# Two output projections of a RetNet and gMLP step recast as Strassen products, with another order of the LayerNorm behind them

## The chip, the core and the metric

The kernel runs on one core of a Trainium2 chip. A core has TensorE (PE in the rows, with its weight loads as PEld), VectorE (DVE), ScalarE (ACT), GpSimd (POOL) and SyncE (SP), which here only issues DMAs. The engines run each their own program and wait for one another on semaphores. The metric is the time on the device in microseconds, as the median of some runs: 1761.06 us before the change (three runs, 1760.05 to 1762.07).

## What is computed

One inference step of two layers, in fp32, for 1024 prompt tokens and 8 decode rows, model width 1024. Layer 1 is retention (four heads, gated), layer 2 a gated MLP of width 2048 with a spatial mix over chunks of 128 tokens. Both end in the same way:

```python
y = (silu(g) * o) @ w_out          # layer 1: [1024, 2048] @ [2048, 1024], the same for 8 decode rows
y = (u * mixed * silu(g)) @ w_out  # layer 2: the same sizes
x = layer_norm(ALPHA * x + y, ln_gain[i], ln_bias[i])
```

These two products are the "output projections". fp32 accuracy comes from splitting each operand into a high part, rounded to the matmul's format, and a low part, the rest; a product is then three matmuls: high by high, high by low, low by high (`mm3`, line 65).

## The kernel before

The order of all instructions is written out by hand (`manual_schedule`); each engine runs its own in that order. SBUF working tiles of 4 KB per partition come from one pool of `NSLOT` = 31 slots (`S`, line 53); an instruction that writes a new tile waits until an older one's last reader is done. PSUM has eight banks of 128x512 (`PS`).

Stages: the input projections of layer 1 (to about 585 us) with the decode state beside them; the retention in chunks (to 750.7); output projection `outb` with LayerNorm (from 750.7); the v projection of layer 2, pieces of `tm_piece` (from 949.6); u and g with the spatial mix, `fm_piece` (from 1146); output projection `outc` with LayerNorm (from 1544.4 to the end).

An output projection (class `OutProj`, lines 627 to 773) runs over four quarters q of the 2048 inner features and two halves n of the 1024 outputs. A piece (q, n) is 512x512 weights. `group` (line 652) multiplies one block of 128 tokens by it: four k-tiles by three terms, 12 matmuls of 512 columns into one bank, which DVE then adds to the tile `pre[tb]`, the residual (lines 662 and 664). `dec_group` does the same for the decode rows, 8 matmuls. So there are 8 pieces of 96 + 8 matmuls. The operands are split while the piece before runs: y by `ysplit` (ACT cast, then a subtraction on DVE or POOL), the weights by `wsplit` (line 123, ACT cast and DVE subtraction). `stream_step` loads and splits the weights of later pieces; `wload` issues the DMAs.

The last quarter is written out (lines 734 to 773): the left half leads the right one by two blocks, and after each right block comes that block's LayerNorm: `bn_stats` of both halves, `bn_aggr`, a power on POOL, `(x - mean) * gain` on DVE (line 702), `* rstd` on ACT (line 704), `+ bias` on POOL (line 708), and a store. In `outb` the finished blocks are transposed on PE (`x1_transpose`, line 782) into the operand of the next stage, some of them between the first groups of its first piece (`hook_x1`). `r_y` and `s_y` are the last transposes and gating of the stage in front, which lie among the first groups of a projection.

DVE's `nb` (line 602, 128x2) belongs to the retention stage: a group-norm bias, behind which ACT and then PE wait.

## Time and profile before

| | us |
|---|---|
| median of three runs | 1761.06 |
| profiled execution, span on the core | 1758.3 |
| PE busy in it | 1726.1 |
| DVE, ACT, POOL busy | 782.3, 537.6, 438.1 |
| `outb`: first matmul to the start of the second `tm` piece | 750.72 to 976.88 |
| `outc`: first matmul to the end of the span | 1544.42 to 1758.3 |
| mean granted TensorE clock | 0.994 |

The profile is of one execution; its span is from the first to the last instruction on the core, and durations are taken from it. A matmul's listed duration overlaps the next one's: how fast they follow one another is read from the starts, or from the chain, which merges a run of them. In the chain a row is the start, the duration and the count of a merged run. DVE instructions overlap by up to 0.1 us in the same way.

### The profile page before, as it was taken

How to read it: one execution, taken by the hardware profiler on the slowest of the kernel's cores; microseconds unless marked ns; L12 is line 12 of the kernel's file. 1: busy time of each engine (PE TensorE's matmuls, PEld its weight loads, DVE VectorE, ACT ScalarE, POOL GpSimd, SP SyncE). 2: the span in 40 equal slices, each digit the busy share in tenths (PEclk: the TensorE clock that was granted, in tenths of full speed). 3: DMA queues.
4: the chain of work that ended last, by engine and by line, in shares of the span. 5: the costliest groups of instructions: out<-in, count | busy, mean ns of one | idle time of the engine just before them, and what ended most of it. 6: DMA issues, size and time to landing. Idle time of an engine off the chain costs nothing.

```text
span 1758.3 us, 22771 instructions
## 1 busy us (share of the span) xinstructions
PE 1726.1 (98%) x9408; PEld 1522.0 (87%) x9408; DVE 782.3 (44%) x1149; ACT 537.6 (31%) x775; POOL 438.1 (25%) x276
## 2 busy tenths in 40 slices
PE   9999999999999999999999999999999999999995
PEld 9898888979999787877778977899999999987774
DVE  7134453533321577753368322154343343333358
ACT  4121424244432454531114222133323333411112
POOL 4122231411101666620026000012222221210116
PEclk9999999999999999999999999999999999999998
DMA  7135565555533544341113322234112221442212
GB/s 265 72 125 192 178 210 193 195 191 205 192 144 121 168 156 156 132 156 49 48 61 122 108 96 77 80 127 160 64 62 95 92 104 73 162 138 92 88 49 97
DMA packets 97703, 223.91 MB, mean 127 GB/s; under 512 B 8296, under 2 KB 43000, under 8 KB 97600
## 3 DMA queue, kind: packets, MB, share of 16 engines
q1 hardware_dynamic: 97392, 222.26, 36.2%
q8 instruction: 74, 1.21, 0.3%
q10 hardware_dynamic: 208, 0.20, 0.0%
q14 instruction: 29, 0.24, 0.0%
HBM read 152.83 MB, written 69.40 MB: 126 GB/s over the span
## 4 chain that ended last, share of the span: by engine, by line
PE 91%; DVE 3%; POOL 2%; issue 2%; DMA 1%; ACT 1%; SPq 0%; DVEq 0%; POOLq 0%; ACTq 0%
PE fm L63 41%; PE tm L63 20%; PE op L63 19%; PE o L63 2%; PE tmd L63 2%; PE pd L63 2%; PE mx L63 1%; PE st L63 1%; PE dps L63 1%; PE yt L1053 1%; DVE pre L702 1%; DVE nb L602 1%; POOL vl L495 1%; DMA qk<-qk_s 1%; PE y L618 1%
## 5 line engine op out<-in xcount | busy, mean ns | idle before, releaser
L63 PE MATMUL fm<-xh,wh 128*128 128x344 f32 x768 | 247.3, 322 | 0.7 <-ACT xh L300 0.7
L63 PE MATMUL fm<-xl,wh 128*128 128x344 f32 x768 | 246.4, 321 | 0.6 <-DVE xl L301 0.5
L63 PE MATMUL fm<-x1h,wh 128*128 128x344 f32 x768 | 246.9, 321 | 0.0
L63 PE MATMUL fm<-xh,wl 128*128 128x344 f32 x768 | 246.2, 321 | 0.0
L63 PE MATMUL fm<-x1h,wl 128*128 128x344 f32 x768 | 245.1, 319 | 0.0
L63 PE MATMUL fm<-x1l,wh 128*128 128x344 f32 x768 | 245.0, 319 | 0.0
L134 DVE TENSOR_TENSOR wl<-wr,wh 128x1024 fp32r<-128x1024 f32 x123 | 171.1, 1394 | 126.8 <-ACT wh L130 108.7
L63 PE MATMUL op<-wh,yh 128*128 128x512 f32 x512 | 202.4, 395 | 0.0
L63 PE MATMUL op<-wl,yh 128*128 128x512 f32 x512 | 201.6, 394 | 0.0
L63 PE MATMUL op<-wh,yl 128*128 128x512 f32 x512 | 201.6, 394 | 0.0
L130 ACT CAST wh<-wr 128x1024 fp32r<-128x1024 f32 x127 | 131.6, 1044 | 211.2 <-PE pd L63 98.0
L63 PEld LDWEIGHTS fm<-xh,wh 128*128 128x128 f32 x768 | 145.2, 189 | 4.7 <-ACT xh L300 1.1
L63 PEld LDWEIGHTS fm<-xl,wh 128*128 128x128 f32 x768 | 145.1, 189 | 2.7 <-DVE xl L301 1.2
L63 PEld LDWEIGHTS fm<-xh,wl 128*128 128x128 f32 x768 | 145.1, 189 | 0.0
L63 PEld LDWEIGHTS fm<-x1h,wh 128*128 128x128 f32 x768 | 144.3, 188 | 0.5
L63 PEld LDWEIGHTS fm<-x1l,wh 128*128 128x128 f32 x768 | 144.3, 188 | 0.4
L63 PEld LDWEIGHTS fm<-x1h,wl 128*128 128x128 f32 x768 | 144.2, 188 | 0.0
L664 DVE TENSOR_TENSOR pre<-pre,op 128x512 f32<-128x512 f32 x96 | 65.6, 684 | 137.6 <-PE op L63 137.6
L63 PEld LDWEIGHTS op<-wh,yh 128*128 128x128 f32 x512 | 96.1, 188 | 23.7
L63 PEld LDWEIGHTS op<-wh,yl 128*128 128x128 f32 x512 | 96.1, 188 | 22.7
L63 PEld LDWEIGHTS op<-wl,yh 128*128 128x128 f32 x512 | 96.1, 188 | 22.2
L412 DVE SCALAR_TENSOR_TENSOR dw<-s,qd_dec,dw 128x512 f32<-128x512 f32 x32 | 39.9, 1246 | 169.6 <-ACT dw L411 169.6
(204 smaller groups left out, 3062.4 us busy)
## 6 DMA issues: line engine op xcount, KB each, us to landing
wr<-in_w SPq DMA_DIRECT2D x127, 512.0 KB
s<-in_state SPq DMA_DIRECT2D x32, 512.0 KB
out_rs<-s SPq DMA_DIRECT2D x32, 512.0 KB
qk_s<-ro SPq DMA_DIRECT2D x16, 512.0 KB
v_s<-v SPq DMA_DIRECT2D x16, 512.0 KB
vbc<-vd_s SPq DMA_DIRECT2D x16, 512.0 KB
g_s<-g SPq DMA_DIRECT2D x16, 512.0 KB
qk<-qk_s SPq DMA_DIRECT2D x16, 512.0 KB
```

What stands on the lines that cost most here:

```text
L63: pe.matmul(out, lhs, rhs, start=start, stop=stop)
L130: act.copy(t, src)
L134: eng.tensor_tensor(t, src, f(W[p][half][0]), ALU.subtract)
L412: dve.scalar_tensor_tensor(w[:, 0, :], s[:, 0, :], qd_dec[:, h, 0, b:b + 1], w[:, 1, :], ALU.mult, ALU.add)
L495: pool.tensor_tensor(ll, src, f(hh), ALU.subtract)
L602: dve.scalar_tensor_tensor(nb, r["mv"][:, :, 0], -1.0, rs[:, 0:2], ALU.mult, ALU.mult)
L618: pe.transpose(ps[:, e * CH + ib * 128:e * CH + (ib + 1) * 128], on[:, ib, (2 * ep + e) * 128:(2 * ep + e + 1) * 128], ident)
L664: dve.tensor_tensor(dst, dst, ps, ALU.add)
L702: dve.scalar_tensor_tensor(t[:, cs], t[:, cs], mv[:np_, 0:1], gain[:, cs], ALU.subtract, ALU.mult)
L1053: pe.transpose(ps[:, k * 128:(k + 1) * 128], q["m"][half][:, k, blk * 128:(blk + 1) * 128], ident)
```

## The change

Each projection is done as two halves s of the inner features. A half is a product of a 2x2 block matrix A (two halves of the tokens by two quarters of features, cells `A(j, k)`) by a 2x2 block matrix B (two quarters of features by two halves of outputs), and is computed by Winograd's form of Strassen's identity: seven block products, p1 to p7, where there were eight. Each is cut into two `subs` c of 256 inner features, 28 subs in all. A sub takes its operands from `prep`: part 0 forms sums and differences of cells in place (on DVE and POOL), part 1 casts both operands on ACT, part 2 subtracts for A's low part on POOL, part 3 for B's on DVE. `prep` runs two subs ahead; for subs 18 to 27 its parts are spread evenly over subs 16 to 23.

In `group` one sub does 4 blocks of 128 tokens by 2 k-tiles by 3 terms. The products are chained in PSUM: p2 has bank set b; p5, then p3, go on in c; p1, p6, p7 and p4 go on in a. After each product DVE adds the bank to the output blocks (`evac`), and the next product of the chain accumulates onto the same bank. The decode rows use p2, p5, p3 and p1 and are added up in SBUF by DVE.

The last four subs (p7 and p4 of the second half) are interleaved by token block in eight steps, with the LayerNorm of all blocks behind them: blocks 0 to 3 are complete in front of the tail, 4 to 7 become complete in it. LayerNorm is now `x * rstd - mean * rstd` on ACT (Identity with bias), then gain and bias as two tensor instructions on DVE and POOL. In `outb` the split of the next weights (piece 32) is on DVE in steps 0 to 3 instead of POOL, and x1's transposes are at other places. In the retention stage the loads and splits of pieces 24 and 25 are replaced by `fetch` and `prep` of the first subs. `outc` reads y back in cells, most of them into the two large buffers that held x1. The pool has 33 slots, and the descriptor scratch of software DMAs is set to 1024 bytes.

The core of the diff, of long stretches the new lines only:

```diff
+NSLOT = 33
...
+    PROJ = (*range(24, 32), *range(56, 64))
+    HOLD_LOAD, HOLD_SPLIT = (*PROJ, 32, 33), (*PROJ, 32)
...
     class OutProj:
+        ORDER = ("p2", "p5", "p3", "p1", "p6", "p7", "p4")
+        CHAIN = {"p2": "b", "p5": "c", "p3": "c", "p1": "a", "p6": "a", "p7": "a", "p4": "a"}
+        OUT = {"p2": (0, 0), "p5": (1, 1), "p3": (0, 1), "p1": (0, 0), "p6": (0, 1), "p7": (1, 1), "p4": (1, 0)}
+        ACELL = {"p2": (0, 1), "p5": (1, 0), "p3": (0, 1), "p1": (0, 0), "p6": (1, 0), "p7": (0, 0), "p4": (1, 1)}
+        BCELL = {"p2": (1, 0), "p5": (0, 1), "p3": (1, 1), "p1": (0, 0), "p6": (0, 1), "p7": (0, 0), "p4": (1, 0)}
...
+            self.subs = [(s, x, c) for s in range(2) for x in self.ORDER for c in range(2)]
...
+        def fetch(self, i):
...
+            s, x, c = self.subs[i]
+            for k in {"p2": ((1, 0),), "p5": ((0, 1), (0, 0)), "p3": ((1, 1),)}.get(x, ()):
+                t = self.b[s, k, c] = S(f"wr{self.p0}_{s}{c}_{k[0]}{k[1]}", (128, 2, 512))
+                sp.dma_start(t, a["w"][self.p0 + 2 * (2 * s + k[0]) + k[1], c])
+        def prep(self, i, part=None):
...
+            s, x, c = self.subs[i]
+            def A(j, k):
+                return self.cell(s, j, k, c)
+            def B(j, k):
+                return self.b[s, (j, k), c]
+            def sub(eng, out, in0, in1):
+                eng.tensor_tensor(out, in0, in1, ALU.subtract)
+            if part == 0:
+                if x == "p5":
+                    pool.tensor_tensor(A(1, 0), A(1, 0), A(1, 1), ALU.add)
+                    sub(dve, B(0, 1), B(0, 1), B(0, 0))
+                if x == "p3":
+                    sub(dve, A(1, 0), A(1, 0), A(0, 0))
+                    sub(pool, A(0, 1), A(0, 1), A(1, 0))
+                if x == "p6":
+                    sub(dve, B(0, 1), B(1, 1), B(0, 1))
+                if x == "p7":
+                    sub(pool, A(0, 0), A(1, 1), A(1, 0))
+                    sub(dve, B(0, 0), B(0, 1), B(0, 0))
+                if x == "p4":
+                    sub(dve, B(1, 0), B(1, 0), B(0, 1))
+                return
+            src = A(*self.ACELL[x]), B(*self.BCELL[x])
+            if part == 1:
+                hl = []
+                for n, t in zip("yw", src):
+                    hl.append([S(f"{n}{k}{self.p0}_{i}", (128, 2, 512), F32R) for k in "hl"])
+                    act.copy(hl[-1][0], t)
+                self.op[i] = hl
+            else:
+                hh, ll = self.op[i][part - 2]
+                sub(pool if part == 2 else dve, ll, src[part - 2], f(hh))
...
+        def group(self, i, pair):
+            s, x, c = self.subs[i]
+            ch = self.CHAIN[x]
+            first = c == 0 and x in ("p2", "p5", "p1")
+            if first:
+                self.ps[ch, pair] = PS(f"op{self.p0}_{s}{ch}_{pair}")
+            ps = self.ps[ch, pair]
+            (ah, al), (bh, bl) = self.op[i]
+            sl = slice(pair * 128, (pair + 1) * 128)
+            for k in range(2):
+                mm3(ps, ah[:, k, sl], al[:, k, sl], bh[:, k, :], bl[:, k, :], first and k == 0, c == 1 and k == 1,
+                    skip=x not in ("p2", "p5", "p1"))
+        def evac(self, i, pair):
+            x = self.subs[i][1]
+            j, n = self.OUT[x]
+            tb = 4 * j + pair
             dst = self.pre[tb][:, n * 512:(n + 1) * 512]
+            ps = self.ps[self.CHAIN[x], pair]
+            if (tb, n) not in self.seen:
+                self.seen.add((tb, n))
                 dve.scalar_tensor_tensor(dst, dst, ALPHA, ps, ALU.mult, ALU.add)
             else:
                 dve.tensor_tensor(dst, dst, ps, ALU.add)
...
         def dec_pre(self, n):
...
+            r8 = small.tile([NB, 512], F32, tag="r8", name=f"r8pd{self.p0}_{n}")
+            dve.tensor_tensor(r8, self.acc[n][:8, :], self.t8[n], ALU.add)
+            dve.scalar_tensor_tensor(dst, dst, ALPHA, r8, ALU.mult, ALU.add)
+            self.ln_half(TB, n)
...
+        def ln_stats(self, tbs):
...
+            for i, tb in enumerate(tbs):
+                dve.bn_aggr(mv[:np_, i, :], self.st.pop(tb)[:np_])
+            dve.tensor_scalar(r[:np_, 0, :n], mv[:np_, :n, 1], EPS, None, ALU.add)
+            pool.tensor_tensor(r[:np_, 1, :n], r[:np_, 0, :n], mhalf[:np_, :n], ALU.pow)
...
+            def nb():
+                dve.scalar_tensor_tensor(r[:np_, 2, :n], mv[:np_, :n, 0], -1.0, r[:np_, 1, :n], ALU.mult, ALU.mult)
...
+        def ln_z(self, tb, cuts=1):
+            rs, nb = self.L.pop(tb)
+            t = self.pre[tb]
+            for cs in self.cut(cuts):
+                act.activation(t[:, cs], t[:, cs], AF.Identity, bias=nb, scale=rs)
+        def ln_gain(self, tb, eng):
+            t = self.pre[tb]
+            eng.tensor_tensor(t, t, self.gain[:NB] if tb == TB else self.gain, ALU.mult)
+        def ln_bias(self, tb, eng, fin):
+            t = self.pre[tb]
+            eng.tensor_tensor(t, t, self.bias[:NB] if tb == TB else self.bias, ALU.add)
+            fin(tb, t, slice(0, D))
...
+        def run(self, fin, extra, last, early):
+            tail = len(self.subs) - 4
+            ahead = 16
+            queue = [(i, part) for i in range(ahead + 2, tail + 4) for part in range(4)]
+            done = 0
+            for i in range(tail):
+                s, x, c = self.subs[i]
+                for pair in range(4):
+                    run_later()
+                    if i < 2:
+                        self.pre_load(4 * i + pair)
+                    if i == 2 and pair == 0:
+                        self.pre_load(TB)
+                    if pair == 0:
+                        self.fetch(i + 4)
+                    if i < ahead:
+                        self.prep(i + 2, pair)
+                    else:
+                        to = len(queue) * (4 * (i - ahead) + pair + 1) // (4 * (tail - ahead))
+                        for j, part in queue[done:to]:
+                            self.prep(j, part)
+                        done = to
...
+                    if i == tail - 2:
+                        if pair >= 2:
+                            self.dec_pre(pair - 2)
+                    if i == tail - 1:
+                        if pair == 0:
+                            self.ln_stats([TB])
+                        if pair == 2:
+                            self.nb()
+                            self.ln_z(TB)
+                        if pair == 3:
+                            self.ln_gain(TB, dve)
+                            self.ln_bias(TB, pool, fin)
+                    early(i, pair)
+                    self.group(i, pair)
+                    if c == 1:
+                        self.evac(i, pair)
+                        if s == 1 and x == "p1":
+                            self.ln_half(pair, 0)
+                        if s == 1 and x == "p6":
+                            self.ln_half(pair, 1)
...
+                if s == 1 and x == "p1" and c == 1:
+                    self.dec_fold()
+            self.ln_stats(range(4))
+            for step, (k, pair) in enumerate(((0, 0), (0, 1), (2, 0), (0, 2), (2, 1), (0, 3), (2, 2), (2, 3))):
                 run_later()
+                tb = 4 + pair
+                for c in range(2):
+                    self.group(tail + k + c, pair)
+                self.evac(tail + k + 1, pair)
+                self.ln_half(tb, 0 if k else 1)
+                if step in (0, 3, 5, 7):
+                    self.nb()
+                if k:
+                    self.ln_stats([tb])
+                for z in {0: (0,), 1: (1,), 2: (2,), 3: (4, 3), 5: (5,), 7: (6,)}.get(step, ()):
+                    self.ln_z(z)
+                if step in (0, 1, 2, 3, 4, 5, 7):
+                    self.ln_gain((0, 1, 2, 4, 3, 5, None, 6)[step], dve if step else pool)
+                if step:
+                    self.ln_bias((None, 0, 1, 2, 4, 3, 5, 6)[step], pool, fin)
+                extra(step)
+            self.nb()
+            self.ln_z(7, 2)
+            t = self.pre[7]
+            for cs in self.cut(2):
+                dve.tensor_tensor(t[:, cs], t[:, cs], self.gain[:, cs], ALU.mult)
+                dve.tensor_tensor(t[:, cs], t[:, cs], self.bias[:, cs], ALU.add)
+                if last:
+                    fin(7, t, cs)
+            if not last:
+                fin(7, t, slice(0, D))
...
-    def extra_b(tb):
-        if tb >= 3:
-            x1_transpose()
-        if tb == 7:
-            x1_transpose()
-        if tb == 0:
+    def extra_b(step):
+        if step < 4:
+            wsplit(32, step, eng=dve)
+        if step in (3, 5):
+            x1_transpose(step // 2 - 1)
+        if step == 5:
             wload(33)
...
         r_load(n + 3)
-        if n == NS - 5:
-            wload(24)
-        if n == NS - 4:
-            wload(25)
-        if n >= NS - 4:
-            wsplit(24, n - NS + 4, eng=pool)
-        if n == NS - 1:
-            for t2 in range(4):
-                outb.ysplit(0, t2)
-            outb.pre_load(0)
-            outb.pre_load(1)
+        if NS - 6 <= n < NS - 2:
+            outb.fetch(n - NS + 6)
+        if n >= NS - 2:
+            outb.prep(n - NS + 2)
...
+    def r_last(i, pair):
+        if (i, pair) == (0, 3):
             r_y(NS - 1)
+        if (i, pair) == (21, 3):
+            wload(32)
...
+    x1_transpose(2)
+    x1_transpose(3)
...
     def hook_x1(i):
+        tb = {0: 4, 2: 5, 3: 6, 4: 7, 5: TB}.get(i)
+        if tb is not None:
+            x1_transpose(tb)
...
+    YC, YB = {}, {}
+    def cell_c(s, i, j, c):
+        if (s, i, j, c) not in YC:
+            if s not in YB:
+                YB[s] = xp.tile([128, KT, T], F32, tag="x", name=f"yb{s}")
+            YC[s, i, j, c] = YB[s][:, 4 * j + 2 * c:4 * j + 2 * c + 2, i * 512:(i + 1) * 512]
+        return YC[s, i, j, c]
+    def yload_c(s, i, j, c, own=False):
+        if own:
+            YC[s, i, j, c] = S(f"ly{i}{j}{c}", (128, 2, 512))
+        sp.dma_start(cell_c(s, i, j, c), y_s[2 * s + j][:, 2 * c:2 * c + 2, i * 512:(i + 1) * 512])
+    outc = OutProj(56, cell_c, y1d, x1_s.rearrange("t p d -> (t p) d"), x1d_s, 1)
...
+                if i in (0, 1):
+                    yload_c(0, 0, 1, i, own=True)
+                    outc.fetch(i)
+                if i in (2, 3):
+                    outc.fetch(i)
+                    outc.prep(i - 2)
                 if i == 4:
+                    yload_c(0, 1, 0, 0, own=True)
+                    yload_c(0, 1, 1, 0, own=True)
         fm_piece(40 + 2 * g, x1["h"], x1["l"], ug_evac(g, AF.Gelu, "u"), per_group=hook_u)
...
+    def early_c(i, pair):
+        if i == 0:
+            if pair == 0:
+                for j in (0, 1):
+                    yload_c(0, 1, j, 1)
+            if pair == 1:
+                yload_c(0, 0, 0, 0)
+                yload_c(0, 0, 0, 1)
+            if pair >= 2:
+                s_y(GR - 1, pair - 2)
+        if i == 2:
+            k, c = ((0, 1, 0), (1, 0, 0), (1, 1, 0), (0, 0, 0))[pair], 0
+            yload_c(1, k[0], k[1], 0)
+            yload_c(1, k[0], k[1], 1)
...
-    outc.run(fin_c, lambda tb: None, True, last_y)
+    outc.run(fin_c, lambda step: None, True, early_c)
-    nc = bacc.Bacc("TRN2", target_bir_lowering=False, num_devices=1)
+    nc = bacc.Bacc("TRN2", target_bir_lowering=False, num_devices=1, dynamic_dma_scratch_size=1024)
```

## Rows read from the trace of the kernel before

**Rows 1.** The page: busy time, share and instructions of each engine; the chain that ended last, by engine.

```profile
PE 1726.1 (98%) x9408; PEld 1522.0 (87%) x9408; DVE 782.3 (44%) x1149; ACT 537.6 (31%) x775; POOL 438.1 (25%) x276
...
PE 91%; DVE 3%; POOL 2%; issue 2%; DMA 1%; ACT 1%; SPq 0%; DVEq 0%; POOLq 0%; ACTq 0%
```

**Rows 2.** The chain that ended last, in order of time: start, duration, engine, tile, line and count of a merged run; `op` are the projection's matmuls, `pd` its decode matmuls, `tm` those of the next stage.

```profile
750.72 8.35 PE op L63 x36
...
773.87 1.84 PE pd L63 x8
775.71 22.27 PE op L63 x96
...
799.82 22.21 PE op L63 x96
...
976.88 22.78 PE tm L63 x192
...
1544.42 5.55 PE op L63 x24
```

**Rows 3.** The end of the span: the last matmul and the last DVE instructions of the timeline (start, duration, engine, line, operation, operands, count), and the sum of the windows from 1735 to 1758 (us, then busy time of each engine).

```profile
1738.73 0.39 PE L63 MATMUL op<-wh,yl 128*128 128x512 f32 x1
...
1750.54 2.93 DVE L708 TENSOR_TENSOR pre<-pre,lnb 128x512 f32<-128x512 f32 x2 [0.56 <-ACT pre L704]
...
sum 23.00, PE 4.11 PEld 3.00 DVE 17.11 ACT 4.67 POOL 12.09; mean PE 1.03 PEld 0.75 DVE 4.28 ACT 1.17 POOL 3.02
```

**Rows 4.** The timelines of POOL and DVE at 649 us (retention), at 757 us and in the LayerNorm of the second projection, in order of time within each place; in brackets the idle time in front and what ended it.

```profile
648.90 2.37 POOL L495 TENSOR_TENSOR qkl<-qk,qkh 128x1024 fp32r<-128x1024 f32 x1
648.96 2.32 DVE L602 SCALAR_TENSOR_TENSOR nb<-mv,rsrn 128x2 f32<-128x2 f32 x1 [0.21 <-POOL rsrn L254]
...
756.83 0.16 DVE L602 SCALAR_TENSOR_TENSOR nb<-mv,rsrn 128x2 f32<-128x2 f32 x1 [0.87 <-POOL rsrn L254]
...
1726.82 1.28 DVE L702 SCALAR_TENSOR_TENSOR pre<-pre,lmv,lng 128x1024 f32<-128x1024 f32 x1
...
1731.52 2.39 POOL L708 TENSOR_TENSOR pred<-pred,lnb 8x1024 f32<-8x1024 f32 x1
1732.35 5.53 DVE L702 SCALAR_TENSOR_TENSOR pre<-pre,lmv,lng 128x1024 f32<-128x1024 f32 x1
1733.88 0.54 POOL L254 TENSOR_TENSOR rsrl<-rstl,mhalf 128x1 f32<-128x1 f32 x1
1734.40 2.39 POOL L708 TENSOR_TENSOR pre<-pre,lnb 128x1024 f32<-128x1024 f32 x1
```

**Rows 5.** The timelines of POOL and DVE in the LayerNorm of the first projection: a drain that reads PSUM and SBUF, and statistics that read one tensor.

```profile
921.45 2.40 POOL L708 TENSOR_TENSOR pre<-pre,lnb 128x1024 f32<-128x1024 f32 x1 [1.26 <-ACT pre L704]
922.32 0.67 DVE L664 TENSOR_TENSOR pre<-pre,op 128x512 f32<-128x512 f32 x1
923.03 0.69 DVE L685 BATCH_NORM_STATS2 lst<-pre 128x6 f32<-128x512 f32 x1
```

**Rows 6.** Casts and subtractions of 128x1024: the group of ACT's weight casts (count, busy us, mean ns, idle before), and from the timelines DVE's subtraction beside POOL's and alone, and a POOL instruction that began beside one of DVE.

```profile
L130 ACT CAST wh<-wr 128x1024 fp32r<-128x1024 f32 x127 | 131.6, 1044 | 211.2 <-PE pd L63 98.0 <-PE op L63 57.4 <-DVE wl L134 14.9
...
750.71 2.97 DVE L641 TENSOR_TENSOR yl<-yT,yh 128x1024 fp32r<-128x1024 f32 x1 [0.38 <-ACT yh L640]
...
763.41 1.22 DVE L134 TENSOR_TENSOR wl<-wr,wh 128x1024 fp32r<-128x1024 f32 x1
...
1728.48 3.09 POOL L708 TENSOR_TENSOR pre<-pre,lnb 128x1024 f32<-128x1024 f32 x1
```

**Rows 7.** One decode step on DVE from the timeline, and two groups of ACT instructions (count, busy us, mean ns, idle before): LayerNorm's scaling, and `on`, an Identity with bias and scale.

```profile
912.98 0.68 DVE L679 SCALAR_TENSOR_TENSOR pred<-pred,r8pd 8x512 f32<-8x512 f32 x1
...
L704 ACT ACTIVATE pre<-pre,rsrl 128x1024 f32<-128x1024 f32 x15 | 17.3, 1152 | 78.7 <-POOL rsrl L254 50.8 <-DVE pre L702 27.9
...
L605 ACT ACTIVATE on<-o,nb,rsrn 128x512 f32<-128x512 f32 x32 | 23.2, 775 | 47.6 <-DVE nb L602 47.6
```

**Rows 8.** The chain again: a set of eight transposes of a block of x1, and those of its decode rows.

```profile
927.82 0.87 PE xt L800 x8
...
947.98 0.59 PE xtd L790 x8
```

**Rows 9.** TensorE after a gap in the retention stage: two rows of its timeline, and the window behind it (us, busy time and count of each engine, the granted clock, the DMA share and GB/s).

```profile
609.55 0.33 PE L618 MATMUL y<-ident,on 128*128 128x128 f32 x1 [2.33 <-ACT on L605]
...
611.43 0.63 PE L63 MATMUL o<-sl,qkh 128*128 128x512 f32 x1
...
610.00:615.00 5.00, 4.78 (x18) 3.93 (x19) 3.79 (x7) 1.53 (x3) 1.97 (x2) 0.66 0.43 158
```

**Rows 10.** The timelines of POOL and DVE at the end of the retention stage: a split of weight piece 24 and the `nb` beside it.

```profile
743.00 2.40 POOL L134 TENSOR_TENSOR wl<-wr,wh 128x1024 fp32r<-128x1024 f32 x1
743.07 2.35 DVE L602 SCALAR_TENSOR_TENSOR nb<-mv,rsrn 128x2 f32<-128x2 f32 x1 [0.81 <-POOL rsrn L254]
```

**Rows 11.** SP's DMA issues at the start of the first projection, and the window there (the last three columns are the clock, the DMA share and GB/s).

```profile
750.68 4.10 SPq L647 DMA_DIRECT2D pre<-in_x  x6
...
750.00:755.00 5.00, 5.00 (x24) 4.03 (x23) 4.62 (x6) 1.62 (x2) 5.00 (x2) 1.00 0.98 329
```

More of the change, by code (lines that the diff above doesn't have):

```diff
@@ L681, in ln_half @@
         def ln_half(self, tb, i):
             np_ = NB if tb == TB else 128
[L683 to L684 removed]
+            if tb not in self.st:
+                self.st[tb] = small.tile([128, 2, 6], F32, tag="lst", bufs=6, name=f"lst{self.p0}_{tb}")
             dve.bn_stats(self.st[tb][:np_, i, :], self.pre[tb][:, i * 512:(i + 1) * 512])
[L687 to L692 removed]
@@ L694, in ln_apply @@
-        def ln_apply(self, tb, fin, cuts=1):
-            np_ = NB if tb == TB else 128
-            t, gain, bias = self.pre[tb], self.gain[:np_], self.bias[:np_]
-            mv, rs = self.L[tb]
-            n = D // cuts
-            cut = [slice(i * n, (i + 1) * n) for i in range(cuts)]
-            for cs in cut:
-                dve.scalar_tensor_tensor(t[:, cs], t[:, cs], mv[:np_, 0:1], gain[:, cs], ALU.subtract, ALU.mult)
-            for cs in cut:
-                act.activation(t[:, cs], t[:, cs], AF.Copy, scale=rs[:np_, 0:1])
-            def add(eng):
-                for cs in cut:
-                    eng.tensor_tensor(t[:, cs], t[:, cs], bias[:, cs], ALU.add)
-                    fin(tb, t, cs)
-            return add
@@ new lines, in cut @@
+        def cut(self, n):
+            return [slice(i * (D // n), (i + 1) * (D // n)) for i in range(n)]
+        def ln_z(self, tb, cuts=1):
[10 more added lines that the diff above has]
+            fin(tb, t, slice(0, D))
```

202 lines of the change are left out of this document (60 added, 142 removed).

## Prediction

> **What bounds the kernel now.** I read the page's busy table first, then the chain that ended last, then the two projections in that chain, and last the queues of VectorE (DVE) and GpSimd (POOL) there. TensorE is busy 98% of the span and the chain is 91% PE [rows 1]; inside both projections it is one unbroken run of `op` matmuls, 22.21 to 22.27 us for 96 of them, so 0.232 us for one of 512 columns, with 1.84 us for the 8 decode matmuls behind each quarter [rows 2]. So a matmul taken away is worth its 0.232 us as long as nothing else is late. The exception is the end: the last matmul begins at 1738.73, the span ends at 1758.3, and what runs between them is LayerNorm on DVE, POOL and ACT, with DVE busy 17.11 of 23 us [rows 3]. The retention stage before the first projection is the other place with PE gaps.
>
> DVE and POOL get in each other's way. A DVE instruction that reads two tensors from SBUF doesn't run while a POOL tensor instruction runs: the 128x2 `nb` took 2.32 us beside a POOL subtraction of 2.37 that began 0.06 earlier, and the 128x1024 LayerNorm step at 1732.35 took 5.53 against 1.28 alone, ending only after three POOL instructions [rows 4]. One that reads PSUM and SBUF isn't held: 0.67 us at 922.32 with POOL busy from 921.45 to 923.85, and so are the statistics [rows 5]. I call the first kind two-input work.
>
> The Trainium skill ("SBUF — State Buffer", section "Who interferes with whom") has a rule for this, which speaks against the change: DVE with two SBUF inputs and GpSimd share a port under an exclusive lock, held for a whole instruction. The rows above agree (2.32 for an instruction of 0.16). Without this rule the sum would be the faster rival's below, with it the forecast's.
>
> **The change, part by part.** Durations are those of the profiled execution, span 1758.3; the median of the runs is 1761.06, so 2.8 us lie around the span, and I add them at the end.
>
> *Matmuls.* A projection has 8 quarters of 96 matmuls, 768; after, 28 sub-products of 4 row blocks, 2 k-tiles and 3 terms, 672. The decode matmuls stay at 64 (16 subs x 4). 96 x 0.232 = 22.3 us saved in each projection, 44.5 in both, if PE stays fed. A sub is 24 x 0.232 = 5.57 us, 6.50 with its decode part (0.93, half of 1.84). The first 16 subs take 10 x 6.50 + 6 x 5.57 = 98.4, the next 8 take 6 x 6.50 + 2 x 5.57 = 50.1, the tail's four 22.3. That an accumulation goes on in a bank just drained is shown by no row; from one group of the chain to the next nothing is lost (773.87 + 1.84 = 775.71 [rows 2]) and nothing can be gained, and a drain that comes late is counted below as a stall, so 0.
>
> *Operands.* Every sub splits an A and a B operand: two ACT casts (1.04 [rows 6]), one POOL subtraction, one DVE subtraction. Ten subs of a half also form sums: 10 on DVE and 6 on POOL. On POOL such a 128x1024 takes 2.37 [rows 4] to 3.09 where it waits for DVE; on DVE 1.22 alone, up to 2.97 beside POOL [rows 6]. I take 2.37 and 1.22 and count the waiting by the sum of both. In the first half this fits: a half has 20 POOL x 2.37 = 47 and 24 DVE x 1.22 = 29, 76 in its 85 us of PE. One place doesn't: behind p5 two products with two POOL steps each follow, and the A operand of p3 needs DVE, POOL, ACT, POOL in a row (1.22 + 2.37 + 1.04 + 2.37). DVE reaches p5's third drain some 4.9 us into p3, where PE wants the bank 2.8 us in: 2.1 us of stall, per projection.
>
> *The last eight subs (16 to 23)* prepare ten (18 to 27). POOL: 10 subtractions and 4 sums at 2.37, the decode bias 2.39 and a power 0.54 [rows 4]: 36.1. DVE two-input: 10 + 8 at 1.22, 4 decode steps at 0.68 [rows 7], a gain 1.28: 26. Sum 62 us where PE needs 50.1. The drains (16 x 0.69) and statistics (8 x 0.69) can lie beside POOL [rows 5], so DVE's own 46 isn't the bound; the pair is. DVE works in program order, so p6's last drains and statistics, for which LayerNorm waits, come at 62 after sub 16's start: 11.9 late. Bounds: 52 if POOL runs far ahead through the slots, 72 if each turn is lost (rivals).
>
> *LayerNorm tail.* From there, step by step in DVE's and POOL's orders: POOL a gain and seven biases at 2.37 and five powers at 0.54 [rows 4], 21.7; DVE six gains at 1.28 and four half-steps at 0.68, 10.4; the pair is full for 32, and idle 5.4 while the first drain, statistics, power and ACT's 1.15 run, and before the last ACT step. That is 37.4 to the last bias, and 4.8 to the end (the last DVE instruction of before ends at 1753.5, the span at 1758.3 [rows 3]). PE's last steps hide inside it. ACT's Identity with bias isn't there at 1024: 1.15 by Copy, 1.55 by twice 0.775 of `on` [rows 7]; I take 1.15, the row of its own size.
>
> *Second projection.* 98.4 + 1.7 (two sets of 8 transposes, 0.87 each [rows 8]) + 2.1 + 62 + 37.4 + 4.8 = 206.4. Before, 1544.42 to 1758.3 is 213.9 [rows 2, 3]. Minus 7.5.
>
> *First projection*, to the start of the second `tm` piece at 976.88: now 226.2 [rows 2]. After it there are transposes of x1, in PE's order; the one of block 3 stands in front of the `tm` groups, and waits for that block's bias, which POOL does fourth: 24.4 after DVE's 62 by the same walk, 26.8 with the two DVE splits of the next weights that now lie in the tail (2 x 1.22). Behind it: five sets of transposes at 0.87, the decode one 0.59 [rows 8], eight groups (22.78 [rows 2]) and 1.87 for decode, 29.6. PE has by then idled over 10 us, and after a gap of 2.3 us in the retention stage its granted clock was 0.66 over 5 us, with matmuls at the lower level (1.2 GHz), 0.63 instead of 0.39 [rows 9]: a third of 5 us, 1.7. 98.4 + 0.9 + 2.1 + 62 + 26.8 + 29.6 + 1.7 = 221.5. Minus 4.7.
>
> *Around it.* The four POOL splits of weight piece 24 leave the retention stage (one held `nb` for 2.35 at 743.07 [rows 10]), two POOL splits come: 0 to -2.3, I take -1. Loads: SP runs ahead of PE (six `pre` loads were issued in 4.1 us) at up to 329 GB/s [rows 11], 1.6 us for 512 KB. In the second projection the loads into `yb` wait for the last x1 matmul, and `pre` 1 to 3 stand behind two of them, four of them, and four and a store: at 1.6 each they land 5, 10 and 13 us in, and DVE wants them at 9.3, 10.7 and 12.1. DVE loses 1, which its slack there takes: 0, and 2 at most if the store is late. The smaller descriptor scratch: every transfer here is on the hardware queue, so 0; above, no PE wait on a DMA is in the trace, so a few tenths each on SP would still be hidden.
>
> Sum: -7.5 - 4.7 - 1 = -13.2; 1758.3 - 13.2 + 2.8 = 1747.9, so **1748**. Of 44.5 saved, some 31 is given back, nearly all to the DVE and POOL pair.
>
> **The rivals.**
> *Faster (PE stays the bound).* POOL's casts and sums mostly depend on nothing recent and could run ahead of DVE, so DVE finds the port free: DVE is done at 52, ten earlier in both. For: POOL is only 25% busy over the span. Against: 33 slots; nine `pre`, eight B cells and four operands for each sub in flight leave about four subs. 1748 - 2 x 10 = 1728; a tail that packs better reaches 1724.
> *Slower (DVE loses its turns).* Of the 24 two-input DVE instructions in the last eight subs some 0.6 find POOL busy (36 of 62) and wait 1.3 us each: 46 + 19, and 7 for ACT casts that come behind POOL, gives 72 instead of 62; PE, held by the drains, then loses the tail's rhythm too. Two projections: +20, 1768. It decides against the change from 68.6 on, where the 13.2 are gone. For: 5.53 for a step of 1.28 [rows 4]. Against: POOL too was made to wait: 3.09 instead of 2.39, where DVE had got in [rows 6].
> *No change*: DVE done at 67 to 70, half way, 1758 to 1764.
> *The change doesn't do what it says*: 512-column `op` matmuls not 3 x 448; nothing speaks for it.
>
> **How the numbers follow.** Forecast 0.42 (1738 to 1757), the faster rival 0.18, no change 0.16, the slower one 0.24. A difference of 0.2% (3.5 us) is about what can be told from none. Faster: 0.42 + 0.18 = 0.60; same 0.16; slower 0.24. The faster rival's floor of 1724 and the slower one's 1768 with 2 us for late loads and one more clock dip in each projection (2 x 1) bound the range: 1724 to 1772. The forecast's own is 1738 to 1757.
>
> **What would show it.** Right: `op` matmuls 3 x 448 of the same 0.39 us; PE unbroken to sub 16 but for stalls of about 2 us at p3; PE waiting for DVE's drains around the last eight subs; DVE subtractions of well over 1.22 mean and POOL at 2.4; from the last matmul to the end more than the 19.6 of before. Wrong: PE without waits until the tail (then it is the faster rival); stalls at p6 and p7 of the first half, or waits for slots in ACT's casts or for DMA at the start.

## The result, and the profile after

The changed kernel takes 1784.28 us (median of four runs, 1783.50 to 1785.79), the kernel before 1761.05 beside it: ratio 1.0131, 95% interval 1.0117 to 1.0146. The change costs 23 us; the forecast was 1748 and the range ended at 1772.

The profiled execution has a span of 1781.8. Its page, the lines that answer to [rows 1]; this chain reaches back over the last 96 us only:

```profile
PE 1700.1 (95%) x9216; PEld 1494.0 (84%) x9216; DVE 913.1 (51%) x1208; ACT 585.5 (33%) x820; POOL 605.1 (34%) x331
...
DVE 4%; ACT 0%; PE 0%; issue 0%; ACTq 0%; DVEq 0%
```

The 192 matmuls are gone as forecast, but PE has only 26 busy us less where 44.5 were expected, in part because it runs at its lower clock behind the longer gaps: the 384 matmuls of `op_1a` average 0.42 to 0.44 us where those of `op_0a` take 0.39. DVE has 131 us more, POOL 167. The end is no longer PE's: this chain is almost all DVE.

Where PE waits, from the list of waits (engine, tile and line, releaser; us in total, times, longest):

```profile
PE op_1a L63 <- DVE pre L731: 28.8, 8, 5.3
PE y L619 <- ACT on L606: 14.3, 15, 3.2
PE tm L63 <- DVE x1l L916: 6.8, 1, 6.8
PE op_0c L63 <- DVE pre L729: 4.8, 3, 2.6
PE op_1c L63 <- DVE pre L731: 4.3, 2, 2.2
```

`op_1a` are the products p1, p6, p7, p4 of the second half; line 731 is the drain that frees their bank. Every place but the second is new.

I divide both projections at rows that every version has: the first `op_0b` matmul, the first `op_1c` matmul (start of sub 16), DVE's fourfold `bn_aggr` (the statistics of blocks 0 to 3, behind p6's last drain), and for the first projection the first 512-column `tm` matmul, for the second the end of the span. PE's timeline of after in the second projection, its first and last rows and those with idle time in front:

```profile
1565.07 0.39 PE L63 MATMUL op_0b<-wh,yh 128*128 128x512 f32 x1
...
1593.77 0.47 PE L63 MATMUL op_0c<-wh,yh 128*128 128x512 f32 x1 [0.81 <-DVE pre L729]
...
1600.76 0.50 PE L63 MATMUL op_0c<-wh,yh 128*128 128x512 f32 x1 [2.57 <-DVE pre L729]
...
1670.62 0.40 PE L63 MATMUL op_1c<-wh,yh 128*128 128x512 f32 x1
...
1688.72 0.51 PE L63 MATMUL op_1c<-wh,yh 128*128 128x512 f32 x1 [2.15 <-DVE pre L731]
...
1718.29 0.50 PE L63 MATMUL op_1a<-wh,yh 128*128 128x512 f32 x1 [1.89 <-DVE pre L731]
...
1730.83 0.76 PE L63 MATMUL op_1a<-wh,yh 128*128 128x512 f32 x1 [5.33 <-DVE pre L731]
...
1742.29 0.77 PE L63 MATMUL op_1a<-wh,yh 128*128 128x512 f32 x1 [3.83 <-DVE pre L731]
...
1760.91 0.50 PE L63 MATMUL op_1a<-wh,yh 128*128 128x512 f32 x1 [1.64 <-DVE pre L731]
...
1763.57 0.40 PE L63 MATMUL op_1a<-wh,yl 128*128 128x512 f32 x1
```

Two windows of five us, one around the gap of 2.57 and one behind the gap of 3.83 (the granted clock is the third number from the end; behind the gaps the matmuls take 0.63 us for a while, the lower level, 1.2 GHz):

```profile
1599.80:1604.80 5.00, 4.04 (x11) 2.47 (x12) 3.65 (x3) 2.04 (x3) 4.71 (x2) 0.69 0.02 3
1743.00:1748.00 5.00, 5.00 (x14) 3.84 (x13) 3.82 (x4) 3.48 (x3) 3.63 (x2) 0.50 0.01 3
```

The forecast's terms in these stretches (its first projection ended at the second `tm` piece; that piece, 24.5 in both kernels, is added) and every version's, in us of one profiled execution; b and c are the first and the second projection:

| | subs 0 to 15, b / c | last eight, b / c | b: on to `tm` | c: on to the end | whole b / c | median |
|---|---|---|---|---|---|---|
| before | | | | | 250.6 / 213.9 | 1761.1 |
| forecast | 101.4 / 102.2 | 62 / 62 | 82.6 | 42.2 | 246.0 / 206.4 | 1748 |
| after | 107.4 / 105.6 | 69.7 / 69.7 | 94.0 | 41.4 | 271.2 / 216.7 | 1784.3 |
| e1 weights first | 105.7 / 100.7 | 68.6 / 68.6 | 94.0 | 41.4 | 268.3 / 210.7 | 1777.0 |
| e2 low by ACT | 101.8 / 100.3 | 60.9 / 59.4 | 95.1 | 41.4 | 257.8 / 201.1 | 1754.9 |
| e3 low on DVE | 103.8 / 103.9 | 66.4 / 66.4 | 94.6 | 41.8 | 264.8 / 212.1 | 1773.8 |
| e4 late transposes | 108.5 / 105.6 | 69.6 / 69.7 | 93.9 | 41.4 | 272.0 / 216.7 | 1786.0 |
| e5 x1 earlier | 107.5 / 105.6 | 69.7 / 69.7 | 87.0 | 41.5 | 264.2 / 216.7 | 1778.8 |
| e6 = e1 + e2 | 103.3 / 100.1 | 60.9 / 59.3 | 93.7 | 41.5 | 257.9 / 200.9 | 1755.2 |
| e7 late preps on DVE | 106.3 / 100.5 | 64.7 / 64.8 | 95.0 | 41.4 | 266.1 / 206.7 | 1769.8 |
| e8 four edits | 101.9 / 100.8 | 64.9 / 65.0 | 87.0 | 41.4 | 253.7 / 207.2 | 1757.6 |
| e9 decode in the tail | 107.5 / 106.8 | 63.4 / 63.5 | 102.7 | 48.8 | 273.7 / 219.1 | 1787.8 |
| e10 = e8 + e9 | 101.9 / 100.7 | 59.5 / 59.5 | 93.7 | 48.8 | 255.2 / 209.0 | 1761.3 |
| e11 = e10, earlier | 101.9 / 100.9 | 58.7 / 58.8 | 93.6 | 48.8 | 254.2 / 208.5 | 1759.7 |
| e12 = e8, nb on POOL | 101.9 / 100.6 | 64.9 / 65.2 | 86.0 | 37.4 | 252.8 / 203.3 | 1753.0 |

Where versions have the same code in a stretch, their cells differ mostly by under 0.5, and by 1.4 at most (b on to `tm`, e2 and e6).

What the forecast missed is 25.2 us in the first projection (6.0 + 7.7 + 11.4, rounded), 10.3 in the second (3.4 + 7.7 - 0.8), and the 1 us hoped for around them: 36.5 together, where 1784.3 is 36.3 from 1748. Only the LayerNorm tail of the second projection came out as summed.

### The profile page after: what moved, and what is told of

The parts are those of the page before. It is cut to its first block, busy times and chain, and to the rows that moved or that the text cites. A ratio compares the mean times of both kernels' runs of the same rounds, so it can differ in the third digit from the quotient of the medians.

```text
span 1781.8 us, 22544 instructions
## 1 busy us (share of the span) xinstructions
PE 1700.1 (95%) x9216; PEld 1494.0 (84%) x9216; DVE 913.1 (51%) x1208; ACT 585.5 (33%) x820; POOL 605.1 (34%) x331
## 5 line engine op out<-in xcount | busy, mean ns | idle before, releaser
L134 DVE TENSOR_TENSOR wl<-wr,wh 128x1024 fp32r<-128x1024 f32 x95 | 137.2, 1449 | 125.4 <-ACT wh L130 107.7
L671 DVE TENSOR_TENSOR wl<-wr,wh 128x1024 fp32r<-128x1024 f32 x56 | 113.3, 2028 | 61.9 <-ACT wh L693 61.9
L1133 POOL TENSOR_TENSOR vl<-lv,vh 128x1024 fp32r<-128x1024 f32 x16 | 40.9, 2553 | 261.7 <-ACT vh L1132 261.7
L421 POOL TENSOR_TENSOR dhl<-dw,dhl 128x512 fp32r<-128x512 f32 x32 | 43.2, 1351 | 242.1 <-ACT dhl L420 234.2
L63 PE MATMUL tm<-wh,x1h 128*128 128x512 f32 (+1 forms) x320 | 113.0, 353 | 6.9 <-DVE x1l L916 6.8
L63 PE MATMUL tm<-wl,x1h 128*128 128x512 f32 (+1 forms) x320 | 112.2, 351 | 0.0
L63 PE MATMUL tm<-wh,x1l 128*128 128x512 f32 (+1 forms) x320 | 112.1, 350 | 0.0
L130 ACT CAST wh<-wr 128x1024 fp32r<-128x1024 f32 x95 | 99.0, 1044 | 21.7 <-DMA wr<-in_w 15.7
L63 PE MATMUL tm<-wh,xh 128*128 128x512 f32 x256 | 101.0, 395 | 0.0
```

Of the source, the lines that this page charges most:

```text
L63: pe.matmul(out, lhs, rhs, start=start, stop=stop, skip_group_check=skip)
L130: act.copy(t, src)
L134: eng.tensor_tensor(t, src, f(W[p][half][0]), ALU.subtract)
L421: pool.tensor_tensor(hl[:, 1, :], w, f(hl[:, 0, :]), ALU.subtract)
L671: eng.tensor_tensor(out, in0, in1, ALU.subtract)
L1133: pool.tensor_tensor(ll, t, f(hh), ALU.subtract)
```

## Experiments

Four theories are weighed. P (port): POOL's instructions hold DVE's two-input ones. O (order): DVE idles for ACT's weight cast, which stands behind a y cast that waits for POOL. L (load): DVE has too much work of its own; L2: too much in subs 20 to 23. Q (queue): work that could go ahead stands behind LayerNorm in its engine's order. DVE's rows of after in the last eight subs of the second projection show signs of the first two:

```profile
1677.18 2.61 DVE L671 TENSOR_TENSOR wl<-wr,wh 128x1024 fp32r<-128x1024 f32 x1 [4.54 <-ACT wh L693]
...
1689.18 5.57 DVE L671 TENSOR_TENSOR wl<-wr,wh 128x1024 fp32r<-128x1024 f32 x2
...
1722.33 2.89 DVE L760 TENSOR_TENSOR r8pd<-acc,t8pd 8x512 f32<-8x512 f32 x1
...
1740.35 0.41 DVE L777 BATCH_NORM_AGGREGATE lmv<-lst 128x2 f32<-128x12 f32 x4
```

It idles 4.54 for a cast, and two subtractions of 1.22 take 5.57, a decode sum of 0.68 [rows 7] takes 2.89, beside POOL. (The expectations of e1 to e3 count the last eight subs to the end of the tail's first drain, 71.5 in after, 1.8 later than the table.)

**e1: weights cast first.**

```diff
-                for n, t in zip("yw", src):
...
-                    act.copy(hl[-1][0], t)
+                for n in ((1, 0) if x in ("p5", "p3", "p7") else (0, 1)):
+                    act.copy(hl[n][0], src[n])
```

> ACT casts the weight operand ahead of the y operand in the subs whose y operand is a sum formed on POOL (p5, p3, p7). Before this run the changed kernel shows DVE done with the last eight subs 71.5 us after sub 16's start: some 46 us of its own work, 16 in which its two-input instructions are stretched beside POOL, 9 idle for ACT's weight cast. Theory O (order: the weight cast stands on ACT behind a y cast that waits for POOL's sum): the idle stretches of 4.5 and 3.4 us go, and the stalls of PE at p3 shrink from 1.5 and 3.4 to under 1; both projections together 15 to 22 us less, 1762 to 1769. Theory P (port: POOL's instructions hold DVE): the idle time turns into waiting beside POOL, DVE is done at 67 to 71, and the time is 1775 to 1784. Theory L (DVE has too much work of its own in these subs): nothing changes, 1782 to 1786.

Measured 1777.0, ratio 1.0089 (1.0074 to 1.0104): P's case for the last eight (68.6), O's for p3, whose stalls are gone in both projections. DVE's groups (count | busy us, mean ns | idle before), of after:

```profile
L671 DVE TENSOR_TENSOR wl<-wr,wh 128x1024 fp32r<-128x1024 f32 x56 | 113.3, 2028 | 61.9 <-ACT wh L693 61.9
L671 DVE TENSOR_TENSOR wr<-wr,wr 128x1024 f32<-128x1024 f32 x32 | 68.0, 2126 | 0.0
L671 DVE TENSOR_TENSOR yb<-yb 128x1024 f32<-128x1024 f32 x3 | 3.6, 1209 | 0.0
```

and of e1:

```profile
L671 DVE TENSOR_TENSOR wl<-wr,wh 128x1024 fp32r<-128x1024 f32 x56 | 102.6, 1833 | 40.1 <-ACT wh L694 40.1
L671 DVE TENSOR_TENSOR wr<-wr,wr 128x1024 f32<-128x1024 f32 x32 | 72.7, 2273 | 0.0
L671 DVE TENSOR_TENSOR yb<-yb 128x1024 f32<-128x1024 f32 x3 | 9.1, 3019 | 0.0
```

Idle time for the cast falls by 22 us, and the three sums of `yb`, which ran alone before, now run beside POOL: 3.02 instead of 1.21 us.

**e2: y's low part by ACT** (28 subtractions of each projection are left out, a cast is in their place).

```diff
-                sub(pool if part == 2 else dve, ll, src[part - 2], f(hh))
+                if part == 2:
+                    act.copy(ll, src[0])
+                else:
+                    sub(dve, ll, src[1], f(hh))
```

> The low part of every y operand is written by an ACT cast in place of POOL's subtraction, so the subtraction is left out and POOL keeps the sums and LayerNorm. Theory P: DVE's weight subtractions fall from a mean of 2.03 us to 1.3 to 1.5, DVE is done with the last eight subs 52 to 58 us after sub 16's start instead of 71.5, and the time is 1745 to 1757. Theory O: the two idle stretches of 4.5 and 3.4 us stay, since POOL's sums still stand ahead of the y cast; DVE is done at 67 to 71 and the time is 1775 to 1784. Theory L: 1782 to 1786.

Measured 1754.9, ratio 0.9963 (0.9950 to 0.9976): 29 us less, as P has it. The same DVE instructions, with POOL busy 166 us less:

```profile
L671 DVE TENSOR_TENSOR wl<-wr,wh 128x1024 fp32r<-128x1024 f32 x56 | 70.9, 1267 | 69.0 <-ACT wh L693 67.5 <-PE op_1a L63 1.6
L671 DVE TENSOR_TENSOR wr<-wr,wr 128x1024 f32<-128x1024 f32 x32 | 43.8, 1369 | 0.0
```

The two groups lose 67 us of busy time, their idle time stays: the port is the larger loss. But the last eight take 60 (62 as the expectation counts), not 52 to 58.

**e3: y's low part on DVE**, nothing left out.

```diff
-                sub(pool if part == 2 else dve, ll, src[part - 2], f(hh))
+                sub(dve, ll, src[part - 2], f(hh))
```

> POOL's subtraction for the low part of every y operand moves to DVE, 28 of 1.22 us in each projection, ten of them in the last eight subs. Theory L: DVE has 46 + 12 of its own in these subs and loses what it lost before, done at 80 to 84, the time 1800 to 1810. Theory P: POOL holds DVE for 2.4 with each subtraction that DVE does in 1.22 itself; without them DVE has 58 of its own, some 3 to 5 beside POOL's sums, and is done at 61 to 66, the time 1765 to 1775. Theory O: the two idle stretches stay but are partly filled with the moved work: 1784 to 1795.

Measured 1773.8, ratio 1.0072 (1.0057 to 1.0087): P's case by its time; the last eight, 66.4 (68 as the expectation counts), lie a little above its 61 to 66. DVE gets 56 instructions more, its busy time stays (913.0 against 913.1 on the page), and the kernel takes 10.5 us less. That rules out L as the whole cause: DVE does each in 1.32 to 1.69 on the mean, where POOL needs 2.4 and more.

**e6: e1 and e2 together.**

```diff
+                for n in ((1, 0) if x in ("p5", "p3", "p7") else (0, 1)):
+                    act.copy(hl[n][0], src[n])
...
+                if part == 2:
+                    act.copy(ll, src[0])
```

> Both earlier edits: weights cast first, and the y operand's low part by an ACT cast, so POOL's subtraction is left out. One alone brought the last eight subs from 69.7 to 68.6 (order), the other to 60.9 and 59.4 us (port). If the idle time for ACT's cast is a second loss that only shows once POOL no longer holds DVE, both together bring the last eight to 51 to 55 and the time to 1739 to 1746. If the idle time is no loss of its own (DVE has 46 of its own and the sums' chain on POOL sets the rest), the last eight stay at 58 to 61 and the time is 1749 to 1755.

Measured 1755.2, ratio 0.9970 (0.9958 to 0.9982), not apart from e2: order isn't a second loss in the last eight. What is left there shows in the windows of subs 16 to 19 and 20 to 23 (us, then busy time and count of PE, PEld, DVE, ACT, POOL; granted clock, DMA share, GB/s):

```profile
1652.30:1678.50 26.20, 26.20 (x115) 19.75 (x114) 15.87 (x19) 14.53 (x15) 12.29 (x4) 1.00 0.00 1
1678.50:1711.60 33.10, 29.89 (x128) 22.83 (x126) 28.93 (x40) 15.01 (x15) 1.64 (x2) 1.00 0.10 33
```

and, for the same subs, in those of after:

```profile
1670.62:1699.04 28.42, 26.27 (x114) 19.48 (x113) 20.52 (x16) 9.67 (x10) 19.70 (x7) 1.00 0.00 1
1699.04:1740.35 41.31, 32.19 (x129) 24.23 (x127) 39.67 (x42) 11.63 (x12) 22.81 (x9) 0.92 0.08 26
```

In e6 DVE is busy 15.9 us in the first four subs, where PE needs 26.2, and 28.9 in the next four, with POOL out of them (1.64), where PE needs 2 x 6.50 + 2 x 5.57 = 24.1. Of after's 41.3 there, DVE is busy 39.7: those 28.9 and 10.7 more, beside a POOL that is busy 22.81. And POOL is idle for the other 18.5: the two engines together are not full there, DVE is. The slack of the first four is of no use to the next.

**e7: e1, and the late preparation on DVE.**

```diff
+                late = dve if i >= 18 else pool
...
+                n = part - 2 if i < 18 or x not in ("p5", "p3", "p7") else 3 - part
+                hh, ll = self.op[i][n]
+                sub(pool if n == 0 and i < 18 else dve, ll, src[n], f(hh))
```

> Weights cast first, and for subs 18 to 27 the y operand's sums and low parts on DVE, so that POOL takes no part in the preparation of the last eight subs; the computation is whole. Theory P: DVE has 46 + 14 x 1.22 = 63 of its own there and nothing holds it: last eight 62 to 65 instead of 69.7, first sixteen as with weights first alone, time 1764 to 1769. Theory L (DVE's load alone sets it): the last eight grow to 80 and more, 1795 to 1805. If a chain of sums and casts sets it, 66 as with the low parts alone on DVE, 1771 to 1775.

Measured 1769.8, ratio 1.0051 (1.0036 to 1.0066): last eight 64.7 and 64.8, P's case; the time is 1 us above it. In subs 20 to 23 of the second projection DVE is as full as in after, with POOL almost out of it:

```profile
1687.41:1726.37 38.96, 32.25 (x129) 24.33 (x127) 38.19 (x49) 10.28 (x10) 1.71 (x2) 0.91 0.08 28
```

**e9: the decode rows' LayerNorm in the tail** (on after; their statistics, scaling, gain and bias move to steps 3 to 6 with it).

```diff
-                    if i == tail - 2:
-                        if pair >= 2:
-                            self.dec_pre(pair - 2)
...
+                if step in (1, 3):
+                    self.dec_pre(step // 2)
```

> The changed kernel with one edit: the decode rows' last sums and their LayerNorm (some 6 us of DVE's own work, 8.5 with the 2.9 us that one of them took beside POOL) leave subs 22 and 23 for the tail, where DVE idles 1.1 to 1.3 us at a time for ACT. With weights first and the low parts on ACT, DVE was busy 15.9 of 26.2 us in subs 16 to 19 and 28.9 of 33.1 in subs 20 to 23, where PE's own work is 24. Theory L2 (DVE's own work is uneven: too much in subs 20 to 23): the last eight fall from 69.7 to 61 to 64, the tail grows by 1 to 3, both projections together 9 to 14 less, 1770 to 1775. Theory P alone (the pair's sum sets it, wherever the work stands): the last eight fall by 6 and the tail grows by 5 or 6, so 1782 to 1785.

Measured 1787.8, ratio 1.0149 (1.0132 to 1.0166). The last eight fall by 6.3, to 63.4 and 63.5, but both theories say that. They part at the tails, which grow by 8.7 and 7.4: more than was moved, near P's 5 or 6 and far from L2's 1 to 3, and the time lies above both. So this run doesn't decide for L2; that DVE's own work is uneven stands on the windows of e6. The idle bits that I counted on are no room: PE now waits 7.73 us for one drain in the second tail (before 1763.37), where after's longest wait there is 3.83.

**e4: the retention stage's last transposes three groups later.**

```diff
-        if (i, pair) == (0, 3):
+        if (i, pair) == (1, 2):
             r_y(NS - 1)
```

> The last transposes of the retention stage stand three groups later in PE's order (36 op matmuls ahead of them as in the kernel before, instead of 18). If the 3.23 us that PE waits there, and the matmuls at the lower clock behind it, are the change's own loss: 3 to 5 us less, 1779 to 1781. If the wait only moves, since the first preps of DVE, POOL and ACT hold the rows that the transposes read: 1783 to 1786.

Measured 1786.0, ratio 1.0139 (1.0122 to 1.0155): no gain. PE's wait at `y` is gone, and these are new in p5 and p3 (PE's timeline of e4):

```profile
769.46 0.50 PE L63 MATMUL op_0c<-wh,yh 128*128 128x512 f32 x1 [1.28 <-DVE pre L729]
...
784.62 0.47 PE L63 MATMUL op_0c<-wh,yh 128*128 128x512 f32 x1 [3.33 <-DVE pre L729]
...
791.61 0.50 PE L63 MATMUL op_0c<-wh,yh 128*128 128x512 f32 x1 [1.03 <-DVE pre L729]
```

DVE was late at p3 anyway. Where it isn't, the same edit does pay: from e7 to e8, which differ in it and in e5's edit (that one acts later), subs 0 to 15 fall from 106.3 to 101.9.

**e5: x1's blocks 2 and 3 ahead of the last block's LayerNorm.** Rows of after there, of POOL (the biases of blocks 4 and 3), of PE (its last wait in the tail, the transposes of blocks 2 and 3, its wait in `tm`) and of ACT; PE's wait of 6.77 follows from ACT's late casts:

```profile
953.43 4.73 POOL L802 TENSOR_TENSOR pre<-pre,lnb 128x1024 f32<-128x1024 f32 x2
...
953.69 0.79 PE L63 MATMUL op_1a<-wh,yh 128*128 128x512 f32 x1 [5.03 <-DVE pre L731]
...
957.87 1.91 PE L911 MATMUL xt<-ident,pre 128*128 128x128 f32 x16
...
973.44 0.58 PE L63 MATMUL tm<-wh,x1h 128*128 128x256 f32 x1 [6.77 <-DVE x1l L916]
...
965.26 1.24 ACT L794 ACTIVATE pre<-pre,lrs 128x1024 f32<-128x1024 f32 x1 [7.20 <-DVE lrs L782]
967.86 1.52 ACT L794 ACTIVATE pre<-pre,lrs 128x512 f32<-128x512 f32 x2 [1.36 <-DVE lrs L782]
969.29 2.02 ACT L915 CAST x1h<-xt 128x512 fp32r<-128x512 f32 x4
```

```diff
-        if step in (3, 5):
-            x1_transpose(step // 2 - 1)
+        if step in (3, 5, 6, 7):
+            x1_transpose((3, 5, 6, 7).index(step))
...
-    x1_transpose(2)
-    x1_transpose(3)
```

> In the first projection the transposes of x1's blocks 2 and 3, with their ACT casts and DVE subtractions, stand in the tail's steps 6 and 7, ahead of the last block's LayerNorm, instead of behind it. Theory Q (the queue): PE waited 6.77 us at the first tm group because these casts and subtractions stood on ACT and DVE behind the last block's LayerNorm, which they don't need. Then that wait falls under 1, the stretch from the four-block statistics to the 512-column tm piece falls from 94.0 to 87 to 89 us, and the time to 1777 to 1780; the second projection doesn't change. Rival (LayerNorm itself is late): the wait comes back at the transposes of a later block, and the time is 1782 to 1785.

Measured 1778.8, ratio 1.0102 (1.0085 to 1.0118): Q's case. The casts come 12 us earlier, counted from DVE's fourfold `bn_aggr` (927.98 in after, 930.09 in e5), and PE's wait is 0.59 (rows of ACT and of PE):

```profile
959.14 2.03 ACT L915 CAST x1h<-xt 128x512 fp32r<-128x512 f32 x4
...
962.03 0.39 PE L63 MATMUL tm<-wh,x1h 128*128 128x256 f32 x1 [0.59 <-DVE x1l L916]
```

**e8: four edits, the whole computation.**

```diff
+                for n in ((1, 0) if x in ("p5", "p3", "p7") else (0, 1)):
...
+                late = dve if i >= 18 else pool
...
+        if step in (3, 5, 6, 7):
...
+        if (i, pair) == (1, 2):
```

> The whole computation with four edits: weights cast first, late preparation on DVE, x1's blocks 2 and 3 ahead of the last block's LayerNorm, and the retention stage's last transposes three groups later. If the gains add up: 1784 - 7 (weights first) - 10 (late preparation) - 6 (x1) - 3 (transposes, now that DVE isn't late at p3) = 1758, 1755 to 1761, a little under the kernel before. If the stalls only move between the four places: 1764 to 1772.

Measured 1757.6, ratio 0.9982 (0.9972 to 0.9991): the gains add up.

**e10 and e11: a fifth edit, and preparation spread from sub 10 on.**

```diff
+                if step in (1, 3):
+                    self.dec_pre(step // 2)
...
-            ahead = 16
+            ahead = 10
```

> The four edits that gave 1757.6, and the decode rows' LayerNorm in the tail as a fifth. By theory L2 the last eight fall from 64.9 to 57 to 60, the tail grows by 1 to 2: 1745 to 1750. If the tail's DVE work is what ends last, the gain is given back there: 1753 to 1758.

> The five edits, and the ten preparations of the last subs begin to spread at sub 10 instead of 16, so that subs 10 to 23 prepare 16 subs and the last eight a little over nine instead of ten. If DVE's own work in subs 20 to 23 is still the bound there, a half to one preparation less (1.5 to 3 us) in each projection: 1741 to 1747. If the 33 slots are too few for operands that are made earlier, waits for slots appear on ACT or SP: 1750 or more.

Measured 1761.3, ratio 1.0000 (0.9991 to 1.0009), and 1759.7, ratio 0.9992 (0.9982 to 1.0001). As in e9 the last eight gain what was moved, 5.4, and the tails give back more, 6.8 and 7.4; 1761.3 is above both of e10's ranges. The earlier spread takes 0.8 off the last eight, less than expected; its 1.6 us in the median are within what can't be told from none. The time lies where waits for slots were expected, but e10, without the earlier spread, isn't faster.

**e12: e8, and LayerNorm's shift on POOL.** In e8 the handover in the tail looks like this (DVE, then ACT):

```profile
1737.20 1.53 DVE L785 SCALAR_TENSOR_TENSOR lrs<-lmv,lrs 128x1 f32<-128x1 f32 x1
...
1738.78 1.24 ACT L797 ACTIVATE pre<-pre,lrs 128x1024 f32<-128x1024 f32 x1 [6.72 <-DVE lrs L785]
```

```diff
+            dve.tensor_scalar(r[:np_, 2, :n], mv[:np_, :n, 0], -1.0, None, ALU.mult)
...
+            pool.tensor_tensor(r[:np_, 2, :n], r[:np_, 2, :n], r[:np_, 1, :n], ALU.mult)
...
-                dve.scalar_tensor_tensor(r[:np_, 2, :n], mv[:np_, :n, 0], -1.0, r[:np_, 1, :n], ALU.mult, ALU.mult)
```

> The four edits that gave 1757.6, and LayerNorm's shift (minus mean times rstd) formed on POOL right behind its power instead of on DVE, where these instructions of 0.15 us took 1.4 to 1.7 us beside a bias on POOL, and where ACT's scaling waited for them behind a drain and a statistic. If the tail is a chain of such handovers between DVE, POOL and ACT, each of the four places loses 1 to 1.5 us: the end of the second projection falls from 41.4 to 36 to 38 us after the four-block statistics, the first by 2 to 4, and the time to 1748 to 1753. If the tail is bound by the sum of DVE's and POOL's work (the forecast's walk: 32 of 37.4 us filled by the pair), the saving is the instructions alone, under 1 in each, and one more POOL instruction each time eats it: 1756 to 1759.

Measured 1753.0, ratio 0.9955 (0.9942 to 0.9969) against before: the fastest whole version, 31 us under the change. The second tail falls from 41.4 to 37.4, the chain's case. The first gains only 1.0, not 2 to 4: ACT's last LayerNorm step begins 4.8 us earlier behind the `bn_aggr` there too (37.5 instead of 42.3), but `tm` doesn't follow; why was not tested. The handover now (POOL, then ACT):

```profile
1732.01 0.19 POOL L784 TENSOR_TENSOR lrs<-lrs 128x1 f32<-128x1 f32 x1
...
1732.23 1.24 ACT L798 ACTIVATE pre<-pre,lrs 128x1024 f32<-128x1024 f32 x1 [5.11 <-POOL lrs L784]
```

## Why the prediction was wrong, step by step

- *Matmuls*: right. 192 are gone, the `op` ones are 3 x 448 of 0.39; that an accumulation goes on in a drained bank costs nothing when DVE is in time (e2 and e6: subs 0 to 15 of c in 100.3 and 100.1, against 98.4 + 1.7).
- *The last eight subs*, "Sum 62 us", "DVE's own 46 isn't the bound; the pair is": the step that failed in both projections, 7.7 us each. That POOL holds DVE is the mechanism, but the pair wasn't full: in c POOL is busy 42.5 of the 69.7 us, in subs 20 to 23 only 22.8 of 41.3, while DVE is busy 39.7. There DVE is the bound, with 28.9 of its own (e6), where PE needs 24.1, and 10.7 of being held. The sum over eight subs hid it, as if work could be shifted among them: DVE's own work was near enough over all eight (44.8 in e6; the terms that I named add up to 42.6, not 46), but it has too little to do early, where PE is the bound, and too much late.
- *The rivals*: 69.7 lies in the 67 to 70 of "no change", and neither rival's time came. By its mechanism this is the slower one (DVE done at 72), with a stretch of 19 and 7 for casts behind POOL; after shows DVE busy 60.2 of 69.7 (15.4 more than in e6), the rest idle. I counted 24 two-input instructions there; 10, 8, 4 and 1 are 23. I gave it 0.24, on the ground that POOL was made to wait too. It does wait, 2.61 to 3.05 on the mean for a low part instead of 2.4, and that doesn't give DVE its time back: both are stretched. Its 1768 was short because it priced only these subs.
- *First projection*, the transposes of block 3: they begin behind block 2's at 957.87, 29.9 us after the fourfold `bn_aggr`, not 26.8, and not because PE waits for block 3's bias: it comes straight from the tail's last matmuls, which had waited 5.03 for a drain, and the bias is done at 958.16, before its transposes. That bias is late too, at 30.2; it is the fifth in `run`, not the fourth. Behind them I followed PE's order only; their casts and subtractions stand on ACT and DVE behind the last block's LayerNorm, 7.0 of the 11.4 us missed (e5). The other 4.4 are those 3.1 and 1.3 more behind it.
- *Operands*, "In the first half this fits", 2.1 us of stall: per engine it fits, in order it doesn't. In c the stalls at p3 are 0.81 + 2.57, with a window at clock 0.69 behind them, and go with the cast order (e1). In b there is a wait of 3.23 at `y` that I had not looked for: a group has half the matmuls now, so the transposes placed "after three groups" have half the cover. e4 shows that this one alone is hidden behind p3's.
- *LayerNorm tail*: 42.2 against 41.4, the sum right but not its account, so the fit is partly luck. I had the pair full for 32 us; e12 takes 4.0 us away by moving instructions of 0.15 us, so in c it is a chain of handovers that ends last. ACT's step there takes 1.24, not 1.15. From the last matmul to the end it is 18.2 us, not more than the 19.6 of before, as I had said it would be.
- *Around it*: the -1 doesn't show: the first projection starts at 750.84 instead of 750.72 [rows 2]. But in e4, e5 and e9, the same code up to there, it starts at 752.0 to 752.9, so a term of 1 us can't be told from none.

A saving is there once DVE is relieved: e12, which computes all of it, has 10.6 us less than before in the second projection, and 2.2 more in the first, which has its LayerNorm and x1 in the way of `tm`.

## What to carry to other kernels

Where an engine with a queue of its own feeds another in step, sum each engine's own work, and what the other's hold adds to it, over stretches as short as its program order fixes them, here four subs and not eight; a sum of two engines' times is a bound only where both are full. And follow an added or moved transfer through every engine's order, not only the waiting one's. Before work is given to POOL to spare DVE, compare what it takes on DVE with how long it will hold DVE. A stall that hides behind another shows no gain when it is removed alone; try it again once the other is gone.
